# Attention in pairs of query blocks and fp32 pieces of one kind side by side, in a one-core kernel for a hybrid attention and retention layer

## The chip, the cores and the metric

One core of a Trainium2 chip runs the whole layer as one program. Its engines are TensorE (PE, the matrix engine), VectorE (DVE), ScalarE (ACT), GpSimd (POOL) and SyncE (SP, which issues nearly all DMAs). The metric is the device time of one execution in microseconds (us). Three runs of the kernel before took 1841.9, 1842.5 and 1843.4 us.

## The reference: what is computed

One layer of inference for 512 prompt tokens, 16 learned meta tokens ahead of them, and 8 samples of 4 new tokens each, which share all weights. Cut to what matters here:

```python
u = rms_norm(h, norm_g) @ w_in                    # 2048 -> 12800 columns, split into ten parts
qa, ka = rope(rms_norm(qa)), rope(rms_norm(ka))   # 16 query heads, 4 key heads, 64 wide
s = qa @ ka.T * 64 ** -0.5                        # keys: meta tokens, block before, own block
m = max(max(s), sink); p = exp(s - m)
o_a = (p / (sum(p) + exp(sink - m))) @ va         # samples: meta tokens, 128 cached keys, own 4
o_r = ((qr @ kr.T) * decay) @ vr + (qr @ S) * d   # retention, 8 heads, chunks of 128 tokens
S = g * S + (kr * wk).T @ vr                      # first S from the meta tokens
o_r = group_norm(o_r) * gn_g + gn_b
y = sigmoid(ga) * ((o_a * silu(za)) @ w_pa) + sigmoid(gr) * ((o_r * silu(zr)) @ w_pr)
out = h + y @ w_o
```

Everything is fp32. Outputs are the layer's result for prompt and samples, the last 128 keys and values, and the retention states.

## The kernel before

**Layout.** Activations stand with the model dimension on the partitions, 16 tiles of 128 (`XH`, `XL`), and tokens along the free dimension: 512 prompt, 32 sample, 16 meta. fp32 products are made from fp32r halves: `split` (L156) writes a high half on ACT and the rest on DVE, and a product is high x high + high x low + low x high. A matmul that reads true fp32 (transposes `tr` through L154, the products with `po`, `spo`, `ri`, `ru0`, `rx`) is not split; such a product shows as two instructions in the profile, a transpose as one.

**The stream of work.** `run_jobs` (L504) goes through jobs, 128 output columns of a weight matrix each: key, value, gate and query columns of attention, then the retention's, then gates and output projections in Strassen-like pairs (`Pair`, `pp`). For each the weights come by `run_load` into `wraw`, `run_split` makes `wspl`, and `run_mm` issues the matmuls into `pproj`, six per contraction step. After each step a clock ticks (`clock[0] += 1`) and `side_step` (L479) lets one waiting generator go on. These generators are the side work: attention heads (`pair_side` and one `block_side` for each of a head's four query blocks), samples (`sample_work`, `sample_side`), retention heads (`ret_side`), and the last residual adds (`out_side`). `yield n` puts a generator off by n ticks; `D2`, `D3`, `D4`, `DQ` (L120) are such distances, and at most `NACT` generators are active. So the order on each engine is fixed by the ticks, not by readiness, and an engine waits in order. The side work shares four PSUM banks (`psb`); the jobs have two double banks (`psmain`).

**The opening** is `start` (L246). It loads x in four token blocks and the samples with the meta tokens (`xext`), squares them (`sq`), takes the power on POOL and scales (`norm`), transposes (`make_x`, first for tokens 0 to 255, `half` 0, later for the rest), and runs the first job in two halves of tokens (`cuts`). `j1.ahead` steps of the second job are run on its first half alone. A table `plan` says behind which step the squares and `norm` of a block go.

**Attention.** `block_side` makes the scores of one block for the two heads of a pair (`psc`, four matmuls), masks and reduces on DVE, Exp on ACT (L732), scales on DVE (L739), transposes (`pT`), multiplies with the values (`po`, 64 output partitions per head) and transposes the meta columns (`pM`).

**Samples.** For each sample `sample_work` multiplies each of four key heads' 32 columns with the cached values (L837) and with the new ones (L838), 16 instructions in the profile; `sample_side` then transposes the sum (`pf`).

**The end.** `out_pair` (L1521) starts `out_side` behind the last step of a pair: ten transposes (`pout`), the residual adds and three stores.

Of the kernel before, what the change touches and what calls it, by code (L numbers as in the profile page):

```python
# [110 lines left out]
def hybrid_step(ctx: ExitStack, tc: tile.TileContext, A, O):  # L111
# [6 lines left out]
    NACT = 4  # L118
    LAG = 2
    D2, D3, D4, DQ = 2, 4, 3, 5  # L120
# [92 lines left out]

    def norm(i):
# [3 lines left out]
        nc.vector.tensor_reduce(out=r, in_=ss[:, i], axis=AX.X, op=ALU.add)  # L218
        rsqrt(r, r, 1.0 / D, 1e-6, 1)
# [26 lines left out]
    def start(j0, j1):  # L246
# [10 lines left out]
        load_ext()  # L257
        load_x(3)
        run_load(j1, 1)
# [5 lines left out]
        for i in range(2):  # L265
            for c in range(4):
                sq(i, c)
            norm(i)
        for j in (j0, j1):
            j.cuts = ((0, 256), (256, TF))  # L270
# [3 lines left out]
        plan = {2: "20 21", 4: "22 23", 6: "n2", 9: "40 41", 10: "42 43", 11: "n4", 14: "30 31", 15: "32 33"}  # L274
        for k in range(NK):
# [4 lines left out]
            for o in plan.get(k, "").split():  # L280
                if o[0] == "n":
                    norm(int(o[1]))
# [12 lines left out]
        for k in range(j1.ahead):  # L295
            run_mm(j1, k, (0,))
        for k in range(NK):
# [3 lines left out]
            if k in (8, 13):  # L301
                run_split(j1, {8: 2, 13: 3}[k])
# [24 lines left out]
    class Job:  # L327
        def __init__(self, w, c0, nk, rhs, n, evac, pre=None, need=None, kdone=None):
            self.w, self.c0, self.nk, self.rhs, self.n, self.evac = w, c0, nk, rhs, n, evac
            self.pre, self.need, self.kdone, self.cuts, self.ahead = pre, need, kdone, None, 0  # L330
            self.banked, self.tile = False, None
# [110 lines left out]
    def run_split(job, s, eng=nc.vector):  # L442
# [5 lines left out]
        wt = spl.tile([P, 2, 4, P], F32R, tag="spl", name="wspl")  # L448
        hi, lo = wt[:, 0], wt[:, 1]
# [177 lines left out]
    def k_side(n, raw):  # L627
# [5 lines left out]
        for i in range(4):  # L633
# [3 lines left out]
            if i < 3:  # L637
                nc.tensor.transpose(o[:, c + P:c + 144], kt[NS:48, 4], ident[NS:48, NS:48])
        tr(pe[:, :48], kt[:48, 4], 48)
# [40 lines left out]
    def pair_side(i, raw, get_sz):  # L680
# [8 lines left out]
        tr(pe[:, :NS], kt[:NS, 4], NS)  # L689
# [15 lines left out]
        for blk in range(4):  # L705
            side_add(block_side(i, blk, Q, st, get_sz))

    def block_side(i, blk, Q, st, get_sz):
        g = i // 2
        nkeys = 272 if blk else 144  # L710
        c0 = 144 * (blk - 1) if blk else 0
        m0 = 0 if blk else 144
        ko, mo = (144, P) if blk else (0, P)
        tt = slot(name="ptile")
        pt3 = r3(tt[:, :2 * nkeys], nkeys)
        mx = sm.tile([P, 2], F32, name="mx")
# [860 lines left out]
```

## Time and profile before

| what | value |
|---|---|
| three runs | 1841.9, 1842.5, 1843.4 us |
| the profiled execution | 1842.4 us, its span 1840.5 us |
| mean granted TensorE clock | 0.997 |
| PE busy | 1810.9 us, 14483 instructions |
| PEld (weight loads) busy | 1767.5 us |
| DVE, ACT, POOL busy | 1219.8, 731.4, 173.5 us |
| PE waits above 0.5 us in total | for `xin` 9.5, gains 7.2, `xh` 2.0, `xl` 1.8 + 1.0, `vmt` 1.1, `ptile` 0.7, `kt` 0.6, `wspl` 0.6 us |

The span runs from the first to the last instruction of the profiled execution; the rest of its time lies around it. Matmuls overlap, so the time one holds the queue is read from the start of the next, not from its own length: of `pproj` with 272 columns each takes about 0.29 us and a new one starts every 0.125 us. A row of the timeline has its start, its length, the engine, the line, the tiles (written <- read), rows x columns of the stationary operand, the moving operand's shape, and a count. A bracket gives the idle time before it and what ended it.

### The profile page before, as it was taken

To read this page: it belongs to the slowest core of one execution; us is meant where nothing else is said; L and a number is where in the kernel's file an instruction comes from. 1 tells how busy PE (TensorE), PEld (TensorE's weight loads), DVE (VectorE), ACT (ScalarE), POOL (GpSimd) and SP (SyncE) were. 2 spreads that over 40 slices of the span, in tenths; PEclk is the share of its full clock that TensorE was granted. 3 is DMA by queue.
4 is the path that set the end of the run, shared out by engine and by line. 5 is a ranking of instruction groups with operands and counts; after the bars stand their busy time and mean duration, and the time that the engine had idled before them with its cause. 6 is when DMAs were issued, how large, how long until landed. Compare 5 with 4: busy or idle time off the path is not lost.

```text
span 1840.5 us, 35155 instructions
## 1 busy us (share of the span) xinstructions
PE 1810.9 (98%) x14483; PEld 1767.5 (96%) x14483; DVE 1219.8 (66%) x2191; ACT 731.4 (40%) x1297; POOL 173.5 (9%) x240
## 2 busy tenths in 40 slices
PE   5999999999999999999999999999999999999999
PEld 4999999988999999999999999999999999999998
DVE  5636666645556555545697767777676678799776
ACT  5535555433323222233344444444444333344332
POOL 1100101100223212222000000000000000120000
PEclk8999999999999999999999999999999999999999
DMA  6232133231534443434454554444447764564553
GB/s 189 73 99 64 52 103 85 75 106 42 180 103 130 133 132 110 126 108 137 146 149 141 151 148 126 117 123 127 143 140 251 228 184 146 153 177 129 141 141 96
DMA packets 358368, 239.53 MB, mean 130 GB/s; under 512 B 12320, under 2 KB 332224, under 8 KB 358176
## 3 DMA queue, kind: packets, MB, share of 16 engines
q1 hardware_dynamic: 358208, 237.29, 44.1%
q8 instruction: 114, 1.87, 0.4%
q14 instruction: 46, 0.38, 0.1%
HBM read 197.27 MB, written 41.88 MB: 130 GB/s over the span
## 4 chain that ended last, share of the span: by engine, by line
PE 92%; DVE 3%; DMA 2%; ACT 1%; issue 1%; SPq 1%; POOL 0%; DVEq 0%; ACTq 0%
PE pproj L471 43%; PE pp L410 38%; PE ro L1137 1%; PE pp L471 1%; DVE wspl L158 1%; PE po L764 1%; DMA qdc<-c_qdec 1%; PE pout L154 0%; PE pT L154 0%; DVE ml L158 0%; PE rso L1097 0%; PE px L154 0%; PE rsu L1103 0%; PE psc L721 0%; PE pM L154 0%
## 5 line engine op out<-in xcount | busy, mean ns | idle before, releaser
L471 PE MATMUL pproj<-xh,wspl 128*128 128x272 f32 (+3 forms) x3840 | 714.6, 295 | 2.0 <-ACT xh L242 2.0
L158 DVE TENSOR_TENSOR wspl<-wraw,wspl 128x512 fp32r<-128x512 f32 (+1 forms) x492 | 465.0, 950 | 218.4 <-ACT wspl L157 215.6
L471 PEld LDWEIGHTS pproj<-xh,wspl 128*128 128x128 f32 x3840 | 567.4, 190 | 11.1 <-issue 4.8
L157 ACT ACTIVATE wspl<-wraw 128x512 fp32r<-128x512 f32 (+1 forms) x492 | 389.0, 804 | 371.5 <-DVE wraw L368 156.7
L471 PE MATMUL pproj<-xl,wspl 128*128 128x272 f32 (+3 forms) x1920 | 405.1, 290 | 1.0 <-DVE xl L243 1.0
L471 PEld LDWEIGHTS pproj<-xl,wspl 128*128 128x128 f32 x1920 | 305.4, 189 | 1.8 <-DVE xl L243 1.8
L410 PE MATMUL pp<-xfh,wspl 128*128 128x272 f32 x1280 | 246.2, 287 | 0.0
L410 PEld LDWEIGHTS pp<-xfh,wspl 128*128 128x128 f32 x1280 | 202.7, 188 | 0.0
L410 PE MATMUL pp<-xh,wspl 128*128 128x272 f32 x960 | 187.6, 288 | 0.0
L410 PE MATMUL pp<-xfl,wspl 128*128 128x272 f32 x640 | 162.8, 287 | 0.0
L410 PEld LDWEIGHTS pp<-xh,wspl 128*128 128x128 f32 x960 | 153.0, 188 | 0.0
L410 PE MATMUL pp<-fh,wspl 128*128 128x272 f32 x768 | 146.3, 288 | 0.2 <-ACT wspl L157 0.2
L410 PE MATMUL pp<-xl,wspl 128*128 128x272 f32 x480 | 123.0, 288 | 0.0
L410 PEld LDWEIGHTS pp<-fh,wspl 128*128 128x128 f32 x768 | 121.2, 188 | 0.6 <-ACT wspl L157 0.3
L410 PEld LDWEIGHTS pp<-xfl,wspl 128*128 128x128 f32 x640 | 120.7, 189 | 0.0
L410 PE MATMUL pp<-fl,wspl 128*128 128x272 f32 x384 | 98.1, 288 | 0.0
L410 PEld LDWEIGHTS pp<-xl,wspl 128*128 128x128 f32 x480 | 90.3, 188 | 0.0
L471 PE MATMUL pproj<-fh,wspl 128*128 128x272 f32 x512 | 84.9, 287 | 0.0
L368 DVE TENSOR_TENSOR wraw<-wraw 128x1024 f32<-128x1024 f32 x64 | 78.0, 1219 | 0.0
L410 PE MATMUL pp<-ofh,wspl 128*128 128x272 f32 x384 | 75.3, 290 | 0.0
L410 PEld LDWEIGHTS pp<-fl,wspl 128*128 128x128 f32 x384 | 72.3, 188 | 0.0
L471 PEld LDWEIGHTS pproj<-fh,wspl 128*128 128x128 f32 x512 | 72.2, 188 | 0.0
(314 smaller groups left out, 2445.9 us busy)
## 6 DMA issues: line engine op xcount, KB each, us to landing
wraw<-w_in SPq DMA_DIRECT2D x200, 512.0 KB
wraw<-w_branch_ret SPq DMA_DIRECT2D x32, 512.0 KB
wraw<-w_out SPq DMA_DIRECT2D x32, 512.0 KB
state<-state_ret SPq DMA_DIRECT2D x16, 512.0 KB
o_ret_sample<-state SPq DMA_DIRECT2D x16, 512.0 KB
wraw<-w_branch_attn SPq DMA_DIRECT2D x16, 512.0 KB
m1l<-m_scr SPq DMA_DIRECT2D x20, 272.0 KB
r_scr<-rprime SPq DMA_DIRECT2D x16, 272.0 KB
```

The costliest lines, as they stand in the source:

```text
L157: nc.scalar.activation(out=hi, in_=src, func=AF.Copy)
L158: eng.tensor_tensor(out=lo, in0=src, in1=hi.bitcast(F32), op=ALU.subtract)
L368: eng.tensor_tensor(out=out, in0=a, in1=b, op=ALU.add)
L410: nc.tensor.matmul(job.ps[bank], w[:, k], job.rhs(form, k)[q], start=fresh and i == 0, stop=i == len(seq) - 1, skip_group_check=True)
L471: nc.tensor.matmul(ps[h][:, :c1 - c0], w, x[:, c0:c1], start=a, stop=e)
L764: nc.tensor.matmul(o, src, PT[:, j * 256 + rh:j * 256 + rh + P], start=("s", j) not in st, stop=False, skip_group_check=True)
L1137: nc.tensor.matmul(o, w[:, cs], x, start=q == 0, stop=q == 5)
```

## The change

- **Blocks in pairs.** `block_side` takes two query blocks: both blocks' scores, one maximum and one sum for four columns, four Exp, two transposes' tiles, then `po` of both and both `pM` side by side. Distances become D2 = 3, D3 = 5, D4 = 5, and three generators are active, not four.
- **Samples.** The values become the stationary operand at full width: two products of 32 columns per sample. What belongs to the new tokens is collected (`spx`) and multiplied by two products at the end. The transposes `pf` go.
- **Shapes.** In `pair_side` and `k_side` the transpose of the extra tokens is a full 128 x 128 one, and the three 16-row ones stand in a row.
- **Retention.** The scores `ri` go up beside `rk`, `rva` of both halves stands with `rvb` and `rx`, `rot` of both halves together. The first state comes from three fp32r products in place of one fp32 product (`kmt`, `vmt` are replaced by `kml`, `vml`).
- **Opening.** `norm` is cut into `rstd` (sum and power) and the scaling. The low halves of six weight pieces are made on POOL, not on DVE; the third piece of the second job is split earlier than before. `j1.ahead` is 16, not 8, for which two pieces of the second job take tiles of `kk` (`spare`). Its second weight load is issued ahead of the fourth block of x.
- **Last stores.** `out_last` takes the place of `out_side` in the last pair: it starts one step earlier, with a delay of 4 ticks, and stores in five pieces.

```diff
-    NACT = 4
+    NACT = 3
-    D2, D3, D4, DQ = 2, 4, 3, 5
+    D2, D3, D4, DQ = 3, 5, 5, 5
...
+    def rstd(i):
+        r = xrs[:, i:i + 1]
+        nc.vector.tensor_reduce(out=r, in_=ss[:, i], axis=AX.X, op=ALU.add)
+        rsqrt(r, r, 1.0 / D, 1e-6, 1)
...
+        run_load(j1, 1)
         load_x(3)
-        run_load(j1, 1)
...
+        j1.spare = 2
...
-        plan = {2: "20 21", 4: "22 23", 6: "n2", 9: "40 41", 10: "42 43", 11: "n4", 14: "30 31", 15: "32 33"}
+        plan = {4: "20 21", 7: "22 23", 9: "r2", 10: "n2 40 41", 12: "42 43", 13: "r4 30 31", 14: "n4 32", 15: "33"}
...
             if k in (1, 5, 8):
-                run_split(j0, {1: 1, 5: 2, 8: 3}[k])
-            if k in (11, 13):
-                run_split(j1, {11: 0, 13: 1}[k])
-        norm(3)
+                run_split(j0, {1: 1, 5: 2, 8: 3}[k], nc.gpsimd)
+            if k in (9, 11, 13):
+                run_split(j1, {9: 0, 11: 1, 13: 2}[k], nc.gpsimd)
+        rstd(3)
         for k in range(NK - LAG, NK):
             run_mm(j0, k, (0,))
+        j1.ahead = 16
+        run_split(j1, 3)
+        norm(3)
+        for k in range(j1.ahead):
+            run_mm(j1, k, (0,))
         for k in range(3):
             make_x(k, 1)
-        j1.ahead = 8
-        for k in range(j1.ahead):
-            run_mm(j1, k, (0,))
...
-        tr(pe[:, :NS], kt[:NS, 4], NS)
+        tr(pe[:, :P], kt[:, 4])
...
-        for blk in range(4):
-            side_add(block_side(i, blk, Q, st, get_sz))
+        for b0 in (0, 2):
+            side_add(block_side(i, b0, Q, st, get_sz))
...
+        for bi, blk in enumerate(blks):
+            for src, rh in ((V4v[:, max(blk - 1, 0), gs], 0), (V4v[:, blk, gs], P)):
+                if rh == 0 and blk == 0:
+                    continue
+                for j in range(2):
+                    o = po[64 * j:64 * j + 64, blk * P:blk * P + P]
+                    nc.tensor.matmul(o, src, PTs[bi][:, j * 256 + rh:j * 256 + rh + P],
+                                     start=("s", j) not in st, stop=False, skip_group_check=True)
+                    st["s", j] = True
         pM = psb("pM")
-        tr(pM[:, :P], pc.rearrange("p v j c -> p (v j c)"))
+        for bi in range(2):
+            tr(pM[:, P * bi:P * bi + P], pcs[bi].rearrange("p v j c -> p (v j c)"))
...
-            for g in range(4):
-                o = po[32 * g:32 * g + 32, 64 * b:64 * b + 64]
-                nc.tensor.matmul(o, PT[:, 32 * g:32 * g + 32], vcv[:, bb, 64 * g:64 * g + 64], start=True, stop=False)
-                nc.tensor.matmul(o, PT[:48, P + 32 * g:P + 32 * g + 32], vx[:, 64 * g:64 * g + 64],
-                                 start=False, stop=True)
+            for q in range(2):
+                nc.tensor.matmul(pov[:, q, b], vcv[:, bb, P * q:P * q + P], ptv[:, q, :, 0:16],
+                                 start=first and q == 0, stop=False, skip_group_check=True)
...
+        for q in range(2):
+            nc.tensor.matmul(po[:, 256 * q:256 * q + 256], vx[:, P * q:P * q + P], st["px"][:48, 256 * q:256 * q + 256],
+                             start=False, stop=True, skip_group_check=True)
...
-        nc.tensor.matmul(pu[:, :256], kmt[96:128], vmt[96:128])
+        for q, (w, x) in enumerate(((kst, vst), (kst, vml), (kml, vst))):
+            nc.tensor.matmul(pu[:, :256], w[96:128], x[96:128], start=q == 0, stop=q == 2)
...
+    def out_last(n, y, x):
...
+        for b in range(2):
+            for j in range(2):
+                tr(pt[:, 0, 256 * b + P * j:256 * b + P * j + P], y[j][:, P * b:P * b + P])
+        yield 3
+        nc.vector.tensor_tensor(out=x[0][:, :512], in0=pt[:, 0], in1=x[0][:, :512], op=ALU.add)
+        nc.sync.dma_start(O["y_prompt"][0, 0:256, cs].rearrange("(b p) c -> p b c", p=P), r3(x[0][:, :512], 256))
+        for j in (1, 0):
+            while not done.get("last") and j == 0:
+                yield 1
...
+            nc.sync.dma_start(ysm[:, n * P + P * j:n * P + P * j + P], x[2][:NS, c])
...
+            if n == NK - 2:
+                if s == 5:
+                    side_add(out_last(n, t["y"], t["x"]), 4)
+                if s == 6:
+                    done["last"] = True
+            elif s == 6:
                 side_add(out_side(n, t["y"], t["x"]), 4)
```

**Where instructions move.** Three places; in each the rows of before come first, then those of the change. A row is the line, the operation, written <- read, and the shape.

TensorE, attention of one head pair: `po` is the product with the values, `pM` the meta columns' transpose, `pproj` the projection that runs meanwhile.

```order
L764 MATMUL po<-PT,v4a 64x128 x2
L154 MATMUL pM<-ident,pc 128x128
L471 MATMUL pproj<-xh,wspl 128x272 x2
L471 MATMUL pproj<-xl,wspl 128x272 x2
L471 MATMUL pproj<-xh,wspl 128x272 x2
L764 MATMUL po<-PT,v4a 64x128 x4
L154 MATMUL pM<-ident,pc 128x128
L471 MATMUL pproj<-xh,wspl 128x272 x2
L471 MATMUL pproj<-xl,wspl 128x272 x2
L471 MATMUL pproj<-xh,wspl 128x272 x2
L764 MATMUL po<-PT,v4a 64x128 x4
L154 MATMUL pM<-ident,pc 128x128
```

```order
L786 MATMUL po<-PT,v4a 64x128 x6
L154 MATMUL pM<-ident,pc 128x128 x2
L479 MATMUL pproj<-xh,wspl 128x272 x2
L479 MATMUL pproj<-xl,wspl 128x272 x2
L479 MATMUL pproj<-xh,wspl 128x272 x2
L786 MATMUL po<-PT,v4a 64x128 x8
L154 MATMUL pM<-ident,pc 128x128 x2
```

Four blocks' `po` and `pM` (the fourth stands 22 rows further in the program before) are now two groups; between a head's last `psc` and its `pT` of the second pair stand 60 matmuls of `pproj`.

VectorE, in the opening's loop: `xrs` is the sum that the scaling of `xin` needs, `xl` the low half of a transposed x tile, `xjunk` the squares, `wspl` a weight piece's low half.

```order
L243 SCALAR_TENSOR_TENSOR xl<-px,gains,xh 128x256
L158 TENSOR_TENSOR wspl<-wraw,wspl 128x512
L243 SCALAR_TENSOR_TENSOR xl<-px,gains,xh 128x256
L218 TENSOR_REDUCE xrs<-xss 128x1
L198 TENSOR_SCALAR xrs<-xrs 128x1
L225 TENSOR_SCALAR xin<-xin,xrs 128x512 x3
L243 SCALAR_TENSOR_TENSOR xl<-px,gains,xh 128x256 x2
L158 TENSOR_TENSOR wspl<-wraw,wspl 128x512
```

```order
L246 SCALAR_TENSOR_TENSOR xl<-px,gains,xh 128x256 x3
L211 SCALAR_TENSOR_TENSOR xjunk,xss<-xin 128x512
L246 SCALAR_TENSOR_TENSOR xl<-px,gains,xh 128x256 x2
L216 TENSOR_REDUCE xrs<-xss 128x1
L198 TENSOR_SCALAR xrs<-xrs 128x1
L246 SCALAR_TENSOR_TENSOR xl<-px,gains,xh 128x256
L228 TENSOR_SCALAR xin<-xin,xrs 128x512 x3
L211 SCALAR_TENSOR_TENSOR xjunk,xss<-xext 48x512
L246 SCALAR_TENSOR_TENSOR xl<-px,gains,xh 128x256 x2
```

The sum and the scaling, one behind the other before, have a tile's `xl` between them, and the weight pieces are no longer in the row.

The end of the program: TensorE, then SyncE's stores (`oy` is the last pair's result, `xres` and `xs` the residuals of prompt and samples).

```order
L410 MATMUL pp_11717<-mh,wspl 128x272
L410 MATMUL pp_11717<-ml,wspl 128x272
L410 MATMUL pp_11717<-mh,wspl 128x272 x8
L154 MATMUL pout<-ident,oy 128x128 x8
L154 MATMUL pout<-ident,oy 32x128 x2
```

```order
L415 MATMUL pp_11451<-mh,wspl 128x272
L415 MATMUL pp_11451<-ml,wspl 128x272
L415 MATMUL pp_11451<-mh,wspl 128x272 x8
L154 MATMUL pout<-ident,oy 128x128 x6
L154 MATMUL pout<-ident,oy 32x128
L154 MATMUL pout<-ident,oy 128x128 x2
L154 MATMUL pout<-ident,oy 32x128
```

```order
L363 DMA wraw<-w_out 128x8x128
L1500 DMA o_y_prompt<-xres 128x2x256 x2
L1504 DMA o_y_sample<-xs 32x256
L1481 DMA xres<-x_prompt 128x2x256 x2
L1484 DMA xs<-x_sample 32x256
L1500 DMA o_y_prompt<-xres 128x2x256 x2
L1504 DMA o_y_sample<-xs 32x256
```

```order
L1506 DMA xres<-x_prompt 128x2x256 x2
L1509 DMA xs<-x_sample 32x256
L1521 DMA o_y_prompt<-xres 128x2x256
L1532 DMA o_y_prompt<-xres 128x2x128
L1534 DMA o_y_sample<-xs 32x128
L1532 DMA o_y_prompt<-xres 128x2x128
L1534 DMA o_y_sample<-xs 32x128
```

All of the last pair's transposes still stand behind its last `pp`; there are five stores in place of three.

More of the change, by code (lines that the diff above doesn't have):

```diff
@@ L447, in run_split @@
         src = r3(job.raw[s // 2], P)[:, 4 * (s % 2):4 * (s % 2) + 4]
-        wt = spl.tile([P, 2, 4, P], F32R, tag="spl", name="wspl")
-        hi, lo = wt[:, 0], wt[:, 1]
+        if s < 4 - job.spare:
+            wt = spl.tile([P, 2, 4, P], F32R, tag="spl", name="wspl")
+            hi, lo = wt[:, 0], wt[:, 1]
+        else:
+            hi, lo = (r3(att.tile([P, TF], F32R, tag="kk", name="wspk", bufs=8)[:, :512], P) for _ in range(2))
         split(hi, lo, src, eng)
@@ L636, in k_side @@
             tr(o[:, c:c + P], kt[:, i])
-            if i < 3:
-                nc.tensor.transpose(o[:, c + P:c + 144], kt[NS:48, 4], ident[NS:48, NS:48])
-        tr(pe[:, :48], kt[:48, 4], 48)
+        tr(pe[:, :P], kt[:, 4])
+        for i in range(3):
+            c = 144 * (i % 2) + P
+            nc.tensor.transpose(pk[i // 2][:, c:c + 16], kt[NS:48, 4], ident[NS:48, NS:48])
         nc.vector.tensor_copy(kxT[:, n], pe[:, :48])
@@ new lines, in block_side @@
+        gs = slice(g * 64, g * 64 + 64)
+        blks = (b0, b0 + 1)
+        nk = [272 if blk else 144 for blk in blks]
+        mx, nmx, es, sums = (sm.tile([P, 4], F32, name=q) for q in ("mx", "nmx", "es", "sums"))
+        pts = []
+        for bi, blk in enumerate(blks):
+            nkeys = nk[bi]
+            c0 = 144 * (blk - 1) if blk else 0
+            m0 = 0 if blk else 144
+            pts.append(r3(slot(name="ptile")[:, :2 * nkeys], nkeys))
+            for j in range(2):
+                q = 2 * bi + j
+                ps = psb("psc")
+                lq = Q[j][:, blk * P:blk * P + P]
+                nc.tensor.matmul(ps[:, :nkeys], lq, KH[g][:, c0:c0 + nkeys], start=True, stop=False)
+                nc.tensor.matmul(ps[:, :nkeys], lq, KL[g][:, c0:c0 + nkeys], start=False, stop=True)
+                nc.vector.tensor_tensor_reduce(out=pts[bi][:, j], in0=ps[:, :nkeys], in1=mask[:, m0:m0 + nkeys],
+                                               scale=0.125, scalar=sinkb[:, 2 * i + j:2 * i + j + 1],
+                                               op0=ALU.add, op1=ALU.max, accum_out=mx[:, q:q + 1])
+            yield 2
@@ new lines, in block_side @@
+        nc.vector.tensor_scalar(out=nmx, in0=mx, scalar1=-1.0, scalar2=None, op0=ALU.mult)
+        nc.vector.tensor_tensor(out=es.rearrange("p (b j) -> p b j", j=2),
+                                in0=sinkb[:, 2 * i:2 * i + 2].unsqueeze(1).to_broadcast([P, 2, 2]),
+                                in1=mx.rearrange("p (b j) -> p b j", j=2), op=ALU.subtract)
+        for q in range(4):
+            nc.scalar.activation(out=pts[q // 2][:, q % 2], in_=pts[q // 2][:, q % 2], func=AF.Exp,
+                                 bias=nmx[:, q:q + 1], accum_out=sums[:, q:q + 1])
@@ L995, in ret_side @@
         tr(pe[:, :P], reps[0])
+        pi = psb("ri")
+        for c in range(4):
+            cs = slice(c * P, c * P + P)
+            nc.tensor.matmul(pi[:, cs], kT[:, cs], qT[:, cs])
         kwh, kwl = r2k(F32R, "kwh"), r2k(F32R, "kwl")
```

179 lines of the change are left out of this document (81 added, 98 removed).

## The prediction

> **What bounds the kernel now.** I read the page first: the span, then the chain of work that ended last.
>
> ```profile
> span 1840.5 us, 35155 instructions
> ...
> PE 92%; DVE 3%; DMA 2%; ACT 1%; issue 1%; SPq 1%; POOL 0%; DVEq 0%; ACTq 0%
> ```
>
> The profiled execution took 1842.4 us (1.9 around its span), 0.1 under the median of the runs shown, 1842.5; the sum is made against 1842.4. TensorE (PE) carries 92% of the chain, so what counts is how long each PE instruction holds the queue, and where PE waits. The table of PE's waits is short; its first row and the row on the softmax are these (total, times, longest):
>
> ```profile
> PE px L154 <- DVE xin L225: 9.5, 3, 3.3
> ...
> PE pT L154 <- DVE ptile L739: 0.7, 2, 0.5
> ```
>
> So there are two ways to gain: the waits, nearly all in the opening, and the small matmuls between the projection's (`pproj`, `pp`). The projection's own count is the same in both programs, 12624.
>
> **The small matmuls.** I price a group of small matmuls by what it adds to the stream: from the start of the projection row ahead of it to the start of the second row behind it, less what the two projection rows take alone. In the PE timeline (start, us) two rows of `pproj` with x2 stand 0.25 us apart, 0.125 a matmul.
>
> ```profile
> 250.91 0.44 PE L764 MATMUL po<-PT,v4a 128*64 128x128 f32 x4
> 251.28 0.33 PE L154 MATMUL pM<-ident,pc 128*128 128x128 f32 x1
> ...
> 286.80 0.41 PE L471 MATMUL pproj<-xh,wspl 128*128 128x272 f32 x2
> 287.14 0.66 PE L764 MATMUL po<-PT,v4a 128*64 128x128 f32 x8
> 287.73 0.33 PE L154 MATMUL pM<-ident,pc 128*128 128x128 f32 x1
> 287.81 0.49 PE L471 MATMUL pproj<-xh,wspl 128*128 128x272 f32 x2
> 288.15 0.29 PE L471 MATMUL pproj<-xl,wspl 128*128 128x272 f32 x1
> ```
>
> *Pairs of blocks (`po`, `pM`).* From 286.80 to 288.15 are 1.35 us; less 0.50 the group costs 0.85. Eight `po` take 0.59 to `pM`, four took 0.37, so four cost 0.22. What eight do not explain is 0.85 - 0.44 = 0.41, of which `pM`, a transpose, is 0.11 (below). So 0.30 is paid once per group for going into the half-width form and out: 0.34 in place of 0.25 stands both at its entry and at its exit. 32 groups become 16: 16 x 0.30 = **-4.8 us**; the bounds are 0.09 (one edge alone) and 0.30, so -1.4 to -4.8. Transposes show no such fee, so joining `pT`, `rva` and `rot` is worth 0.
>
> ```profile
> 402.17 0.30 PE L837 MATMUL spo<-kvc,sPT 128*32 128x64 f32 x2
> ...
> 403.99 0.44 PE L154 MATMUL pkc<-ident,kvc 128*128 128x128 f32 x2
> ...
> 468.23 1.05 PE L1012 MATMUL ri<-rot 128*128 128x128 f32 x8
> 469.04 0.50 PE L471 MATMUL pproj<-xh,wspl 128*128 128x280 f32 x2
> ```
>
> *Sample values (`spo`).* A sample's 16 instructions, all 32 columns wide, take 1.82 us, with the entry 1.92; eight samples 15.4. They become two full-width fp32 products, four instructions in the profile. Full-width fp32 runs in `ri` at 0.81 / 8 = 0.10 us, with the exit 0.11: four are 0.44, eight samples 3.5. Behind them come two products of 256 columns over 48 rows, which no row shows; by the `ru` rows below 1.4. The four transposes `pf` go (0.44). Sum 15.4 + 0.4 - 3.5 - 1.4 = **-10.9**. If a full-width instruction with so few columns cost what one of the 16 does (0.114) it is the same; if twice that, -7.3.
>
> ```profile
> 299.20 0.60 PE L154 MATMUL pq<-ident,kt 128*128 128x128 f32 x4
> 299.73 0.24 PE L154 MATMUL pqe<-ident,kt 32*128 32x32 f32 x1
> 299.91 0.52 PE L471 MATMUL pproj<-xh,wspl 128*128 128x272 f32 x2
> ```
>
> *Transposes of odd shape.* `pq` and `pqe` take 0.71 and an exit of 0.09, 0.80; five full ones 5 x 0.11 = 0.55. Eight heads: -2.0. In `k_side` three 16-row transposes stood between full ones, now in a row: per group two changes of shape fewer on each side and a full `pke`, an estimate by `pqe` of 0.6, twice: -1.2. Together **-3.2** (-2 to -4).
>
> ```profile
> 535.91 0.69 PE L1069 MATMUL ru<-vmt,kmt 32*128 32x256 f32 x2
> 536.54 0.53 PE L471 MATMUL pproj<-xh,wspl 128*128 128x280 f32 x2
> ```
>
> *First state (`ru`).* One fp32 product is two instructions: 0.63, with edges of 0.09 each 0.81. Three fp32r products replace it. At the pace of the projection (0.12) they are 0.36 + 0.18 = 0.54; at the pace of today's two, 1.14. I take the first, since fp32r passes once: 8 x -0.27 = **-2.2** (-2.2 to +2.6).
>
> **The opening.**
>
> ```profile
> 17.00:43.70 26.70, 18.97 (x104) 16.15 (x103) 18.93 (x49) 14.88 (x36) 1.80 (x4) 0.81 0.61 165
> ...
> 35.89 0.47 PE L154 MATMUL px<-ident,xin 128*128 128x128 f32 x1 [2.93 <-DVE xin L225]
> ```
>
> The first row is a stretch: from the first projection matmul (17.0) to the first of 304 columns (43.7) PE is busy 18.97 of 26.7 us; 0.81 is the granted clock. Idle are 7.7. A clock of 0.81 is 10 us at half speed (0.19 x 26.7 / 0.5); the wait of 2.93 lies among them, and the other 7 would take half, 3.5. So about 11 can be won at most. The change takes five weight subtractions off DVE (0.69 each, below) to POOL, runs `rstd` a step ahead of `norm`, so that DVE doesn't stand in front of POOL's power, and puts 24 more matmuls of the second job (24 x 0.12 = 2.9 us) where PE waited for `xin`. x3 arrives later, behind a 512 KB weight load, but its squares come only at the loop's end. What stays: the first two steps at half clock (three matmuls and two transposes each, 1.2 lost) and a lag of DVE. I take **-9**; ends -3 (only the extra matmuls) and -11.
>
> ```profile
> L158 DVE TENSOR_TENSOR wspl<-wraw,wspl 128x512 fp32r<-128x512 f32 x56 | 38.4, 688 | 25.0 <-ACT wspl L157 24.9
> ...
> L1027 POOL TENSOR_TENSOR innl<-inn,innh 128x512 fp32r<-128x512 f32 x8 | 10.3, 1288 | 15.6 <-ACT innh L1026 15.6
> ...
> 462.20 2.46 DVE L158 TENSOR_TENSOR wspl<-wraw,wspl 128x512 fp32r<-128x512 f32 x2
> ...
> 462.32 1.79 POOL L954 TENSOR_TENSOR rot<-rot,rtmp 128x544 f32<-128x544 f32 x1 [14.11 <-DVE rtmp L953]
> ```
>
> What speaks against: POOL needs 1.29 us for such a subtraction, and two DVE subtractions that ran beside a POOL one took 2.46 instead of 1.38. Six on POOL are 7.7 us; if they meet DVE's squares and scalings for half or more of that, DVE is 4 to 6 us later. [...]
>
> **The last stores.** (DVE, SP issue and PE, in order of time.)
>
> ```profile
> 1834.76 1.57 PE L154 MATMUL pout<-ident,oy 128*128 128x128 f32 x10
> 1834.96 0.44 DVE L429 TENSOR_TENSOR oy<-pp,oy 128x272 f32<-128x272 f32 x1 [2.54 <-PE pp L410]
> 1835.40 0.69 DVE L1499 TENSOR_TENSOR xres<-pout,xres 128x512 f32<-128x512 f32 x1
> ...
> 1836.12 1.36 SPq L1500 DMA_DIRECT2D o_y_prompt<-xres  x2
> ...
> 1837.57 0.41 SPq L1504 DMA_DIRECT2D o_y_sample<-xs  x1
> ```
>
> The new order lets the first transposes only after the last matmul of the step (its delay of 4 ticks is the step's whole length), so nothing is stored earlier. The first store is ready as before, at 1836.1; then SP issues five in place of three, some 0.45 apart (0.41 for one, and a gap): the last at 1837.9, not 1837.6. **+0.4** (-0.5 to +0.8).
>
> **New waits in attention.** Before, three of a head's four blocks came to Exp together and the fourth later; now all four come together.
>
> ```profile
> 276.15 0.41 ACT L732 ACTIVATE ptile<-ptile,nmx 128x144 f32<-128x144 f32 x1 [4.46 <-DVE nmx L729]
> ...
> 279.27 0.62 ACT L157 ACTIVATE wspl<-wraw 128x512 fp32r<-128x512 f32 x1
> ...
> 279.40 0.16 DVE L736 TENSOR_TENSOR sums<-sums,es 128x2 f32<-128x2 f32 x1
> 279.59 0.17 DVE L737 RECIPROCAL sums<-sums 128x2 f32<-128x2 f32 x1
> 279.80 0.63 DVE L739 TENSOR_SCALAR ptile<-ptile,sums 128x272 f32<-128x272 f32 x2
> ...
> L723 DVE CUSTOM_DVE_ANT_0 ptile<-psc,mask,sinkb 128x272 f32<-128x272 f32 (+1 forms) x56 | 23.4, 464 | 12.8 <-PE psc L722 12.8
> ```
>
> Three blocks' Exp took 3.12 us; four take about 4.1, with one weight split (0.6) 4.7. Then DVE scales the second pair: sum and reciprocal 0.4, 4 x 0.32. From the last `psc` to the second pair's `pT` the new order has 60 projection matmuls and six transposes, 60 x 0.125 + 6 x 0.11 = 8.2 us; two score reductions (0.46 each), Exp and scaling need 0.9 + 4.7 + 1.7 = 7.3, and a second split on either engine (0.6 to 0.7) uses most of the margin. Behind the waiting DVE instruction stand the next weights' subtractions, behind PE's wait the whole projection. I take **+3** (0.4 a head; 0 to 20). In retention I expect no cost: its groups keep their distances, and no wait of PE for a bank stood there before.
>
> **Sum:** 1842.4 - 4.8 - 10.9 - 3.2 - 2.2 - 9.0 + 0.4 + 3.0 = 1815.7, **1816 us**.
>
> **Rivals.**
> [...]
> - *`pT` waits every head*: 2.6 us eight times, 21 in place of 3: 1834. For it the thin margin of 0.9; against it, before had only 0.7 in all.
> - *The small matmuls keep their price*: half of `spo` and a third of `po` is won, 5.4 and 3.2 lost: 1825. It covers, too, that the change doesn't do what it says.
> - *Slower*: DVE, waiting in order for the eight Exp's sums, holds the subtractions of `wspl`, and the projection itself runs dry in attention. It decides from (26.7 + 3) / 8 = 3.7 us a head; with an Exp table load and two splits caught in between (some 4.2) it gives 34 in place of 3: 1847.
>
> **How the numbers follow.** Forecast 0.58, port 0.17, `pT` 0.12, price 0.09, slower 0.04. The range leaves out `pT` and the slower rival, 0.16, and takes in the others with the ends of the unknown costs: down to 1806 (opening -11, no new waits, the rest a little cheaper than taken) and up to 1830 (the price rival with +5 of waits). About 0.2% (3.7 us) is what a measurement of this kernel can tell from no change; within it only part of the slower rival falls: faster 0.95, same 0.01, slower 0.04.
>
> **What would show it.** `po` in groups of 6 and 8 with `pM` x2 costing 1.2 and 1.4; `spo` x4 in 0.44; the first 304-column matmul near 37.5 (43.7 - 9 + 2.9), with a granted clock of 1.0 from 20 on; PE's waits for `xin` inside that stretch gone; the last store issued near its end, five in a row. Wrong: a row of PE waits for `ptile` or `wspl` above 5 us.

## The result, and the profile after

The changed kernel takes 1820.1 us (median of 4 runs, 1818.8 to 1820.4), the kernel before 1842.9 beside it (1841.9 to 1843.4): a ratio of 0.9875, 95% interval 0.9858 to 0.9892. That is 22.8 us less; the forecast was 1816, 26.5 less than the runs shown then. The profiled execution took 1819.9 us, 22.5 under that of before.

The page of the changed kernel (span; busy time, share and instructions of PE; shares of the chain by engine):

```profile
span 1817.9 us, 34819 instructions
...
PE 1788.9 (98%) x14395; PEld 1763.9 (97%) x14395; DVE 1205.3 (66%) x2082; ACT 722.0 (40%) x1257; POOL 181.7 (10%) x246
...
PE 94%; DVE 3%; DMA 1%; issue 1%; ACT 1%; POOL 0%; SPq 0%; DVEq 0%; ACTq 0%
```

PE carries 94% of the chain now, 92% before. The table of PE's waits (total, times, longest), without `pg` (the first gains, 7.4) and the rows below 0.9:

```profile
PE px L154 <- DVE xin L228: 7.4, 2, 4.1
...
PE rx L1064 <- POOL qpad L1040: 5.1, 1, 5.1
PE pproj L479 <- ACT xh L245: 1.3, 1, 1.3
PE pproj L479 <- DVE xl L246: 1.2, 1, 1.2
PE pk L154 <- DVE kt L633: 0.9, 1, 0.9
```

Three things are to be seen. The softmax's `ptile` has no row at all, so the waits in attention that the forecast feared did not come. There is a new row of 5.1 us, for `rx` in retention, where the forecast had no cost. And the opening, from the first projection matmul to the first of 304 columns, has two waits left, for `xh` and `xl`, 2.5 us together; before it had five there, 7.5 us together (1.8, 0.4 and 0.4 for `xl`, 2.0 for `xh`, 2.9 for `xin`). The 7.4 for `xin` lie ahead of that stretch.

Since both programs have the same 12624 projection matmuls, the n-th of them can be compared between two traces. The difference says how much the kernel has won up to that place (start times in us; the n-th is counted from 0, so the 300th stands right behind the second of the two groups that transpose k):

| | before | after | difference |
|---|---|---|---|
| first projection matmul | 17.0 | 18.1 | +1.1 |
| first of 304 columns | 43.6 | 40.0 | -3.6 |
| 300th projection matmul (opening done) | 86.9 | 80.3 | -6.6 |
| 2600th (attention and samples done) | 474.9 | 444.1 | -30.8 |
| 2700th | 492.9 | 466.7 | -26.2 |
| last | 1834.6 | 1811.9 | -22.7 |
| end of the span | 1840.5 | 1817.9 | -22.6 |

Between the 2600th and the 2700th 4.5 us are lost again: that is the place of `rx`. From the 5400th on the difference changes by 0.4 alone.

**The groups.** In PE's timeline of the changed kernel (start, us) these are a pair of blocks, a sample, and the first state:

```profile
277.11 0.41 PE L479 MATMUL pproj<-xh,wspl 128*128 128x272 f32 x2
...
277.45 1.09 PE L786 MATMUL po<-PT,v4a 128*64 128x128 f32 x16
278.48 0.44 PE L154 MATMUL pM<-ident,pc 128*128 128x128 f32 x2
278.67 0.50 PE L479 MATMUL pproj<-xh,wspl 128*128 128x272 f32 x2
...
279.00 0.41 PE L479 MATMUL pproj<-xl,wspl 128*128 128x272 f32 x2
...
410.78 0.41 PE L479 MATMUL pproj<-xh,wspl 128*128 128x272 f32 x2
411.03 0.53 PE L863 MATMUL spo<-sPT,kvc 128*128 128x32 f32 x4
411.39 0.50 PE L479 MATMUL pproj<-xh,wspl 128*128 128x272 f32 x2
411.72 0.41 PE L479 MATMUL pproj<-xl,wspl 128*128 128x272 f32 x2
...
471.40 0.38 PE L1092 MATMUL ru<-vst,kst 32*128 32x256 f32 x1
471.62 0.28 PE L1092 MATMUL ru<-vml,kst 32*128 32x256 f32 x1
471.74 0.27 PE L1092 MATMUL ru<-vst,kml 32*128 32x256 f32 x1
471.95 0.53 PE L479 MATMUL pproj<-xh,wspl 128*128 128x280 f32 x2
```

The pair costs 279.00 - 277.11 = 1.89, less four projection matmuls (0.50) 1.39. The forecast's price (16 `po` at 0.055, two transposes at 0.11, one fee of 0.30) gives 1.40. The sample costs 0.94 - 0.50 = 0.44, as forecast. The first state's three products start 0.22 and 0.12 apart and the projection goes on 0.21 later, so the group is dearer than 0.54; over all 8 heads its median is 0.74, before 0.83.

**The opening.** A row of the table by stretches (us; busy time and instructions of PE, PEld, DVE, ACT, POOL; granted clock; DMA), from the first projection matmul to the first of 304 columns, then stretches in the opening and behind `rx`:

```profile
18.07:40.00 21.93, 19.38 (x127) 17.93 (x125) 18.08 (x43) 15.42 (x37) 10.64 (x10) 0.92 0.84 226
...
22.00:28.00 6.00, 5.42 (x45) 5.09 (x43) 5.02 (x13) 5.34 (x13) 4.13 (x4) 1.00 1.05 298
28.00:36.00 8.00, 6.04 (x35) 5.84 (x36) 7.40 (x18) 5.30 (x14) 4.13 (x4) 0.79 0.79 203
...
461.70:463.00 1.30, 1.23 (x5) 1.23 (x6) 0.55 (x1) 0.72 (x2) 1.30 (x3) 0.50 1.04 302
463.00:465.00 2.00, 2.00 (x11) 2.00 (x10) 0.14 (x1) 0.00 (x0) 1.92 (x3) 0.50 0.64 167
```

The stretch is 21.9 us long, 26.7 before, with 24 matmuls more in it; the clock is 0.92, not yet 1.0: it stands at 1.00 from 22 to 28 and at 0.79 from 28 to 36. What ran there is seen in the timeline (DVE, POOL and PE):

```profile
26.95 1.26 POOL L158 TENSOR_TENSOR wspl<-wraw,wspl 128x512 fp32r<-128x512 f32 x1
...
27.01 2.28 DVE L228 TENSOR_SCALAR xin<-xin,xrs 128x512 f32<-128x512 f32 x3
...
28.75 0.38 PE L479 MATMUL pproj<-xh,wspl 128*128 128x256 f32 x1 [1.33 <-ACT xh L245]
...
30.35 0.38 PE L479 MATMUL pproj<-xl,wspl 128*128 128x256 f32 x1 [1.21 <-DVE xl L246]
```

Three scalings that take 1.28 without a POOL subtraction beside them (experiment 5) took 2.28 beside one of 1.26: held up by 1.0, and on a scaling with one operand. A second set, at 33.1, took 2.29 beside one of 1.28. TensorE's two waits stand close by, but experiment 5 shows that they do not hang on this hold.

**The new wait.** SP's issues, POOL and PE around `rx` in the first retention head:

```profile
445.07 0.81 SPq L913 DMA_DIRECT2D o_win_k_sample<-cache_win_k  x1
445.92 0.70 SPq L913 DMA_DIRECT2D o_win_v_sample<-cache_win_v  x1
...
447.44 0.43 SPq L993 DMA_DIRECT2D qdc<-c_qdec  x1
...
460.01 1.26 POOL L1036 TENSOR_TENSOR qd<-rot,qdc 128x512 f32<-128x512 f32 x1 [10.38 <-DMA qdc<-c_qdec]
461.21 0.20 POOL L1040 COPY qpad<-rot 128x16 f32<-128x16 f32 x1
...
461.77 0.80 PE L1064 MATMUL rx<-qpad,rep 128*128 128x128 f32 x2 [5.13 <-POOL qpad L1040]
```

The row `qdc` of 64 KB is issued at 447.4, behind two window copies of 992 KB each, and lands at 460, 12.6 us later. POOL's `qd` waits for it, `qpad` stands behind `qd` in POOL's order though it doesn't need it, and `rx` needs `qpad`. In the kernel before the load was as late (issued at 462.8, `qd` began at 475.0), but `rx` stood behind two more yields and came when `qpad` was there. Behind the wait the clock is at half: 3.3 us at 0.50 up to 465, so the wait costs some 1.7 us more than its length (an estimate, 0.5 x 3.3).

### The profile page after: what moved, and what is told of

Read it like the earlier page. It is cut to its first block, busy times and chain, and to the rows that moved or that the text cites. A ratio compares the mean times of both kernels' runs of the same rounds, so it can differ in the third digit from the quotient of the medians.

```text
span 1817.9 us, 34819 instructions
## 1 busy us (share of the span) xinstructions
PE 1788.9 (98%) x14395; PEld 1763.9 (97%) x14395; DVE 1205.3 (66%) x2082; ACT 722.0 (40%) x1257; POOL 181.7 (10%) x246
## 4 chain that ended last, share of the span: by engine, by line
PE 94%; DVE 3%; DMA 1%; issue 1%; ACT 1%; POOL 0%; SPq 0%; DVEq 0%; ACTq 0%
PE pproj L479 45%; PE pp L415 38%; PE ro L1160 1%; PE pp L479 1%; DVE wspl L158 1%; PE po L786 1%; DMA qdc<-c_qdec 1%; PE pT L154 1%; DMA xin<-x_prompt 1%; PE px L154 1%; PE pout L154 0%; DVE ml L158 0%; PE rso L1120 0%; PE psc L735 0%; PE psc L734 0%
## 5 line engine op out<-in xcount | busy, mean ns | idle before, releaser
L479 PE MATMUL pproj<-xh,wspl 128*128 128x272 f32 (+3 forms) x3808 | 696.7, 294 | 1.3 <-ACT xh L245 1.3
L479 PEld LDWEIGHTS pproj<-xh,wspl 128*128 128x128 f32 x3808 | 559.3, 189 | 8.3 <-ACT xh L245 1.5
L373 POOL TENSOR_TENSOR wsum<-wraw 128x1024 f32<-128x1024 f32 x2 | 4.8, 2399 | 704.5 <-DMA m1l<-m_scr 698.1
```

What stands on the lines that cost most here:

```text
L373: eng.tensor_tensor(out=out, in0=a, in1=b, op=ALU.add)
L479: nc.tensor.matmul(ps[h][:, :c1 - c0], w, x[:, c0:c1], start=a, stop=e)
```

## The experiments

Times are medians beside the kernel before on the same chip (1842.1 to 1843.4). Since executions differ by up to 2 us in the pace of the projection alone, local effects are read from the n-th projection matmul.

**1. Window copies behind the first head's loads.**

```diff
-        copy_windows()
         yield 1
...
             Sts.append(r3(t, 256))
+        if h == 0:
+            copy_windows()
```

> The changed kernel with one edit: the two copies of the windows (about 1 MB each) are issued behind the loads of retention's first head instead of ahead of them. Theory: TensorE's new wait of 5.1 us at rx is a late load; the decay row qdc, issued right behind the two copies, landed 12.6 us after its issue, GpSimd's qd waited for it and qpad behind qd. Then qdc lands some 3 us after its issue, TensorE's wait for qpad goes, and the time is 1820 - 5 = 1815 us. Rival: rx simply stands too early in its step and the load would be late in any order, or the weights behind the copies come late instead: a wait of 3 us or more stays in TensorE's table and the time is 1818 to 1820.

Measured 1812.1 us, ratio 0.9832 (0.9818 to 0.9847). SP and POOL in its timeline:

```profile
446.17 0.42 SPq L992 DMA_DIRECT2D qdc<-c_qdec  x1
...
451.28 1.54 POOL L1037 TENSOR_TENSOR qd<-rot,qdc 128x512 f32<-128x512 f32 x1 [2.93 <-DMA qdc<-c_qdec]
```

`qdc` is there 5.1 us after its issue, not 12.6, and the wait for `qpad` is gone from PE's table. From the 2600th to the 2700th matmul this version wins 6.9 us: 5.1 of wait, the rest clock. Of the 8.2 between the two profiled executions (8.0 between the medians) the other 1.3 lie in the opening and are not the edit: the last part of the second block of x landed later in the profiled execution of the changed kernel (`px` for it began at 15.7 there; 14.5 to 14.9 in twelve of the fourteen profiles of this study). Whether the other three executions of the changed kernel had the late load isn't known. This version is the base of most runs that follow.

**2. `rx` put back.**

```diff
-        px = psb("rx")
-        nc.tensor.matmul(px[:, :P], reps[0], qp.rearrange("p a b -> p (a b)"))
         for n in range(2):
...
+        px = psb("rx")
+        nc.tensor.matmul(px[:, :P], reps[0], qp.rearrange("p a b -> p (a b)"))
         r = slice(96, 128)
```

> The changed kernel with one edit: rx goes back behind the two steps of the value halves, where it stood before the change. Theory: the wait of 5.1 us comes from the place of rx alone; some 6 ticks later (about 4.5 us and more) qpad is there, the wait goes, the load of qdc is as late as ever, and the time is 1815 us. Rival: the wait only moves (what is behind the late qd, the products of the query halves, becomes the wait), or rx alone between projection matmuls costs a switch again (8 x 0.3 = 2.4): 1817.5 to 1820.

Measured 1813.6 us, 0.984 (0.9824 to 0.9857). Its rows of PE's waits:

```profile
PE ru L1092 <- DVE vml L1076: 0.9, 1, 0.9
...
PE rx L1074 <- POOL qpad L1040: 0.2, 1, 0.2
```

The place of `rx` alone takes away 5.1 to 0.2; 0.9 come back one step further, and at the 2800th matmul it is 1.9 behind experiment 1. Both theories hold in part: the move made the wait, the late load is its cause.

**3. The two blocks' `po` apart.**

```diff
+        pM = psb("pM")
         for bi, blk in enumerate(blks):
...
-        pM = psb("pM")
-        for bi in range(2):
+            tr(pM[:, P * bi:P * bi + P], pcs[bi].rearrange("p v j c -> p (v j c)"))
```

> The changed kernel with one edit: inside each pair's step the order is po of the first block, its pM, po of the second block, its pM, so that the half-width form is entered and left twice, with as many instructions at the same place. Theory (a fee of 0.30 us per entry into and exit from the half-width form): 16 groups more, 16 x 0.30 = +4.8, 1825 us, and a group of 8 po and its pM apart costs 0.3 more. Rival (the gain came from fewer interruptions of the projection, not from the switches): at most +1, 1820 to 1821.

Measured 1824.1 us, 4.0 more. The same pair in its PE timeline:

```profile
278.05 0.41 PE L479 MATMUL pproj<-xh,wspl 128*128 128x272 f32 x2
278.39 0.66 PE L787 MATMUL po<-PT,v4a 128*64 128x128 f32 x8
278.98 0.33 PE L154 MATMUL pM<-ident,pc 128*128 128x128 f32 x1
279.23 0.66 PE L787 MATMUL po<-PT,v4a 128*64 128x128 f32 x8
...
280.24 0.41 PE L479 MATMUL pproj<-xl,wspl 128*128 128x272 f32 x2
```

2.19 - 0.50 = 1.69 against 1.39: 0.30 for one entry and exit more, as many instructions at the same place. Both kinds of group show it (1.70 for 1.40 and 1.48 for 1.18), 16 x 0.30 = 4.8. By the marks it loses 4.9 between the 300th and the 2600th matmul; the profiled executions differ by less, 3.6, because the late load of x is missing in this one. The fee is shown.

**4. The opening as before.**

```diff
-        j1.ahead = 16
-        run_split(j1, 3)
-        norm(3)
-        for k in range(j1.ahead):
-            run_mm(j1, k, (0,))
+        norm(3)
...
         for k in range(3):
             make_x(k, 1)
+        j1.ahead = 8
+        for k in range(j1.ahead):
+            run_mm(j1, k, (0,))
...
```

> The changed kernel with the opening as before the change (order of loads, norm in one piece, low weight halves on VectorE, 8 matmuls ahead), all else as changed. Theory from the two timelines (the first 304-column matmul came 3.75 us earlier, with 24 matmuls more ahead of it, 2.8 us): the opening won 6.6, so 1820 + 6.6 = 1826.7, with the first 304-column matmul at 43.8. Rival (the prediction's -9 stands and what is missing was lost elsewhere): 1829. Second rival (the later part of the kernel gives the gain back, since the next jobs' weights come at their own pace): 1820 to 1823.

Measured 1823.8 us, 3.7 more than the changed kernel. Its 300th matmul starts at 85.5, 5.3 later than in the changed kernel and 6.5 later than in experiment 1, which has the early load. So the opening is worth about 6.5, less the 1.3 of a late load in this one profile. The time shows less, near what the second rival had, but not for its reason: at the 2700th matmul it is still 5.3 behind, and then comes back bit by bit to 4.1 at the last, since the same matmuls run 0.1% faster in this execution. The transposes of k stand here without the wait for `kt` (groups of 1.53 us, twice); in the changed kernel one of the two waits 0.9 and costs 2.69.

**5. The low weight halves of the opening on VectorE.**

```diff
-                run_split(j0, {1: 1, 5: 2, 8: 3}[k], nc.gpsimd)
+                run_split(j0, {1: 1, 5: 2, 8: 3}[k])
...
-                run_split(j1, {9: 0, 11: 1, 13: 2}[k], nc.gpsimd)
+                run_split(j1, {9: 0, 11: 1, 13: 2}[k])
```

> The version with the window copies late (1812.1) with one edit: the six low weight halves of the opening are made on VectorE instead of GpSimd. [...] What GpSimd's help is worth is only the difference: the first 304-column matmul comes 1 to 2 us later than 38.8, and the time is 1813 to 1814. Rival (the prediction's step, the help counts in full): first 304-column matmul at 42 or later, with the wait for xin of some 2 to 3 us back and a half clock behind it, 1816. Second rival (the help is harm): 1811 or less.

Measured 1810.5 us. The scalings take 1.28 again:

```profile
26.84 1.28 DVE L228 TENSOR_SCALAR xin<-xin,xrs 128x512 f32<-128x512 f32 x3
```

The 300th matmul comes 0.57 later than in experiment 1, less than the 1 to 2 us that were expected, and than the first rival had. The second rival's time, 1811 or less, came, but not through the opening: the 1.9 us are gained bit by bit over the remaining 1700 us, at a pace 0.1% faster, on another chip, and beside the kernel before the two ratios hardly differ (0.9826, interval 0.9812 to 0.9841). Six subtractions moved to GpSimd are worth 0.6 us here, not the 4.1 (6 x 0.69) that they take on VectorE. TensorE's waits in that stretch stay without the hold, 1.2 for `xh` and 1.2 in three parts for `xl`, and so does the granted clock:

```profile
28.00:36.00 8.00, 6.83 (x40) 6.44 (x41) 7.28 (x22) 5.42 (x15) 2.01 (x3) 0.79 0.74 201
```

So the hold is real, but neither these waits nor the clock behind them come from it alone: on VectorE the subtractions (0.69 each) take time in its place.

**6. Eight steps ahead instead of sixteen.**

```diff
-        j1.ahead = 16
+        j1.ahead = 8
```

> The version with the window copies late (1812.1) with one edit: 8 instead of 16 matmul steps of the second job run ahead, so that 24 matmuls (24 x 0.118 = 2.8 us) go back behind the first job's second half. Theory: they fill time in which TensorE would wait for the scaled x3 (its first piece is there at 36.8, TensorE would be done at 34.3): the wait for xin comes back with some 2.6 us, the projection is 2.6 us later from then on and, with a half clock behind a wait of that length, up to 4: 1815 to 1816. Rival: the wait is hidden by other work (the transposes of the first job's second half are there in time): below 1, 1812 to 1813.

Measured 1823.2 us, 11 more: both theories missed. The wait came back as expected (2.59 us), but 10.4 us are lost by the 300th matmul. By stretches, this version and then experiment 1:

```profile
42.00:50.00 8.00, 8.00 (x28) 5.78 (x27) 2.16 (x5) 2.34 (x5) 0.00 (x0) 0.50 0.23 66
50.00:60.00 10.00, 10.00 (x36) 7.39 (x35) 3.20 (x6) 2.80 (x6) 0.00 (x0) 0.50 0.00 0
```

```profile
42.00:50.00 8.00, 8.00 (x48) 6.25 (x48) 4.09 (x9) 4.07 (x8) 0.00 (x0) 1.00 0.23 66
```

The same stage (three matmuls of 304 columns, then two transposes and one of 48 rows) ran at 1.00 in experiment 1, where it was entered so, and stayed at 0.50 for some 20 us here, where it was entered behind the wait, though PE was busy throughout. Its first to last 304-column matmul take 34.6 us in place of 22.0.

**7. Eight steps, but dense matmuls behind the wait.**

```diff
-        j1.ahead = 16
+        j1.ahead = 8
         run_split(j1, 3)
         norm(3)
-        for k in range(j1.ahead):
-            run_mm(j1, k, (0,))
         for k in range(3):
             make_x(k, 1)
+        for k in range(j1.ahead):
+            run_mm(j1, k, (0,))
```

> The version with the window copies late (1812.1) with one edit: 8 steps of the second job run ahead, and the first transposes of the first job's second half stand ahead of them, not behind (the order of before the change). With 8 steps behind the wait for xin the granted clock stayed at 0.50 from 42 to 60 us and the kernel lost 10.4. Theory (it is the stretch of 304-column matmuls with their transposes that doesn't get the clock back once a wait has cost it; dense matmuls do): here 24 dense matmuls lie between the wait and that stretch, the clock is back at 1.0 within some 6 us, the stretch takes about 22 us in place of 34.6, and the 300th projection matmul comes 3 to 4.5 us later than with 16 steps: 1815 to 1817. Rival (the number of steps run ahead decides, the cold clock comes in any order): 10 later, 1822.

Measured 1818.2 us. The wait is longer, the stage is at 1.00:

```profile
38.00:42.00 4.00, 4.00 (x20) 3.62 (x19) 1.07 (x2) 0.81 (x2) 0.00 (x0) 0.52 0.07 19
42.00:50.00 8.00, 8.00 (x52) 6.43 (x50) 3.03 (x6) 3.09 (x6) 0.00 (x0) 1.00 0.09 23
```

The 300th matmul is 5.8 later than in experiment 1, not 10.4 (4.5 was expected at most; the wait is 6.0 here). Behind the wait stand dense matmuls here, and the clock is back at 1.00 at 42, some 6 us later; in experiment 6 it stayed at 0.50 up to 60 in the stage with transposes. Experiment 6 has the other half of this in its own trace: the clock had fallen there too, to 0.79 from 28 to 36, and was back after 3.4 us at 0.50 (0.21 x 8 / 0.5), a stretch of matmuls of 0.58 to 0.63 us with no transpose between them. What the two runs show of the order is its price, 4.6 us; why the clock came back in one and not in the other they don't show.

**8. The first state's products issued twice** (the second three write the same place anew, so the result is the same).

```diff
+        for _ in range(2):
             for q, (w, x) in enumerate(((kst, vst), (kst, vml), (kml, vst))):
```

> The version with the window copies late with one edit: the three products of the first state are issued twice, the second time into the same place from the start, so that the result is the same. Their group costs 0.74 now, and the prediction took 0.54 = 3 x 0.12 + 0.18. Theory (a product costs 0.12 and the switch into and out of 32 rows costs 0.38, not 0.18): three more cost 0.36, the group 1.10, 1812.1 + 8 x 0.36 = 1815. Rival (each product on 32 rows costs 0.25): three more cost 0.74, the group 1.48, 1818.

Measured 1815.5 us (a single run; its second block of x landed late too). PE's timeline:

```profile
464.64 0.27 PE L1094 MATMUL ru<-vst,kml 32*128 32x256 f32 x1
464.76 0.28 PE L1094 MATMUL ru<-vst,kst 32*128 32x256 f32 x1
```

Three more cost 2.8 us over 8 heads by the projection's marks, 0.35 a head: 0.12 each. So a product is as cheap as forecast, and the switch into and out of 32 rows costs 0.74 - 0.36 = 0.38, not 0.18.

**9. Less delay in attention.**

```diff
-    D2, D3, D4, DQ = 3, 5, 5, 5
+    D2, D3, D4, DQ = 3, 3, 5, 5
```

> The version with the window copies late with one edit: the delay from the exponentials to the scaling and from there to pT is two ticks (some 1.5 us) shorter in all (D3 3 in place of 5). Theory (the margin in attention is as thin as the prediction had it, and the waits of 3 us stayed out by half a microsecond): in a head's second pair the first scaled block is there 0.55 us ahead of pT now, so pT waits some 0.9 us in each of 8 heads, 1812.1 + 7 = 1819, with a row of TensorE's waits for ptile near 7. Rival (the margin is wider, the prediction had counted too much into it): no wait above 1 us in all, 1812. Second rival (VectorE stands in order behind the exponentials and the weights' halves come late): TensorE waits for wspl in attention, 1825 and more.

Measured 1826.5 us, 14.3 more. PE's waits:

```profile
PE pT L154 <- DVE ptile L756: 6.5, 8, 0.9
PE rx L1065 <- POOL qpad L1041: 3.5, 2, 1.9
```

The waits for `ptile` are those expected: the margin is thin. The time is near the second rival's, but its row, a wait for `wspl` in attention, is not there. The cost of the waits isn't as expected: the groups of `pT` and the transposes that went with them cost 9.8 us more in all (behind its first wait each `pT` follows the scalings one by one), and in two retention heads `rx`, now earlier against its loads, waits again, 4.1 by its groups.

**10. Warming products.**

```diff
+        pw = psetup.tile([P, 512], F32, tag="px", name="pwarm")
+        wz = vz.rearrange("p a b c -> p (a b c)")
+        for _ in range(5):
+            nc.tensor.matmul(pw, wz[:, :P], wz)
```

> The version with the window copies late with one edit: five fp32 products of zeros by zeros (128x512) that nobody reads are put on TensorE's queue behind the transpose of the gains, in the time in which it waits for the first rows of x (7.5 to 14.7 us). Theory (TensorE's half clock limits the first steps): the granted clock is 1.0 from the first projection matmul on and not from 19.7, and the 300th projection matmul comes 1 to 1.5 us earlier, 1811. Rival (VectorE and ScalarE set the pace of the first steps): the clock is 1.0 there all the same, and the time is 1812. Second rival (the products hold up the first transposes): some 0.5 later.

Measured 1810.8 us, 0.9829 (0.9813 to 0.9846). The 300th matmul comes 0.9 us earlier: near the theory. The first projection matmul, in PE's timeline of this version and of experiment 1:

```profile
16.79 0.39 PE L483 MATMUL pproj<-xh,wspl 128*128 128x256 f32 x1
```

```profile
17.09 0.58 PE L479 MATMUL pproj<-xh,wspl 128*128 128x256 f32 x1
```

It takes 0.39 and not 0.58, though the column of the granted clock has 1.00 for 17 to 20 in both. The trace's record of the clock starts only at 19.3 in experiment 1, at 11.2 here, and the column shows 1.00 where there is no record: for the first matmuls of a run the durations tell.

**11. Sample values as before.**

```diff
-            for q in range(2):
-                nc.tensor.matmul(pov[:, q, b], vcv[:, bb, P * q:P * q + P], ptv[:, q, :, 0:16],
-                                 start=first and q == 0, stop=False, skip_group_check=True)
+            for g in range(4):
+                o = po[32 * g:32 * g + 32, 64 * b:64 * b + 64]
+                nc.tensor.matmul(o, PT[:, 32 * g:32 * g + 32], vcv[:, bb, 64 * g:64 * g + 64], start=True, stop=False)
...
```

> The version with the window copies late with one edit: the sample values as before the change (16 products of 32 columns for each sample, a copy, and four transposes at the end). Theory (the time goes by instructions of TensorE, and the groups in the two traces differ by 11.7 us): 1812.1 + 11.7 = 1823.8. Rival (the prediction's other end: a full-width product of so few columns costs twice what the groups seem to show, or the old group lay beside other work): +7.3 or less, 1819.4.

Measured 1824.8 us, 12.7 more; 1.2 of it is a wait of `rke` for POOL's `rep` that only this version has. The theory's 11.7 stands.

**12. The best version.** Experiments 1 and 10, with the two low halves that ran beside scalings back on VectorE.

```diff
-                run_split(j1, {9: 0, 11: 1, 13: 2}[k], nc.gpsimd)
+                run_split(j1, {9: 0, 11: 1, 13: 2}[k], nc.gpsimd if k == 11 else nc.vector)
```

> The window copies late, the five warming products, and two of the six low weight halves of the opening (those that ran beside the scaling of x2 and of the 48 extra rows) back on VectorE. Theory (a scaling that a GpSimd subtraction holds takes 1.0 us more, the same subtraction on VectorE takes 0.69): the two scalings take 1.28 again, the 300th projection matmul comes 0 to 0.6 us earlier than with the warming products alone, 1810.5. Rival (VectorE sets the pace of the opening by its sum of work, so that the two halves cost it 1.4): 0 to 0.8 later, 1811.5.

Measured 1810.5 us (5 runs, 1810.3 to 1810.9), 0.9826 (0.9813 to 0.9839). The two scalings take 1.28 and 1.27, the 300th matmul comes 0.13 earlier than in experiment 10. It beats both kernels; nearly all of that is experiment 1, and beside the kernel before it can't be told from experiments 1, 5 and 10.

## Why the prediction was right, and where it was wrong

The time lies in the range, and 4.2 us over the forecast when profiled execution is set against sum. Some of that closeness is luck: in the terms below 12.0 us were won less than forecast (retention 6.9, opening 2.7, first state 1.5, `pk` 0.9) and 7.8 more (waits in attention 3.7, all others 4.1), and the two nearly offset each other.

| term of the sum (us) | forecast | measured | from |
|---|---|---|---|
| pairs of blocks | -4.8 | -4.8 | groups; experiment 3 |
| sample values | -10.9 | -11.7 | groups; experiment 11 |
| odd transposes `pq`, `pk` | -2.0, -1.2 | -2.1, -0.3 | groups |
| first state | -2.2 | -0.7, and a wait of 1.2 less | groups; experiment 8 |
| opening | -9.0 | -6.3 (-7.6 without the late load) | the 300th matmul, less `pk` |
| last stores | +0.4 | +0.1 | end of the span less last matmul |
| waits in attention | +3.0 | -0.7 | PE's table |
| retention | 0 | +6.9 | experiment 1 |
| rest, put to no term | | -1.7 | |
| sum | -26.7 | -22.5 | |

- **Small matmuls: right, by the mechanism.** The fee per switch is what the forecast read from one row, 0.30, and full-width instructions cost 0.11 with 32 columns too. The two products over 48 rows took 1.26, 1.4 was taken. So the rival of kept prices fell.
- **First state: the price of a product was right, the fee was mis-sized.** An fp32r product is one instruction of 0.12 in the rows (experiment 8). The forecast took two edges of 0.09; there are four of about 0.1 in the changed kernel's rows (starts 0.35 for 0.25 and 0.22 for 0.12 apart going in, 0.21 for 0.12 and 0.36 for 0.25 coming out), 0.38 in all by experiment 8. The wait of the first head's `ru` for `vmt`, 1.1 in PE's table of before, went with the fp32 copy; the forecast hadn't counted it.
- **Odd transposes:** `pk` would have won 1.5 (experiment 4, 2.27 to 1.53 twice); a new wait of 0.9 for `kt` takes most of it.
- **Opening: 1.4 too much (2.7 with the late load), and in part for another reason than given.** The forecast gave weight to five subtractions off VectorE; experiment 5 prices them at 0.6. The chances have a case "port" (0.17): no run shows a port; what the runs showed in its place are three scalings that take 2.28 beside a POOL subtraction and 1.28 without one, which would have been the answer had the rest been worth nothing. What wins is the order: sixteen steps ahead, for which the forecast had 2.9 us of filled wait, close the wait for `xin`, and so the clock stays at 1.00 in the stage in which it stood at 0.50 for some 20 us in experiment 6. With eight steps in the order of before 5.8 of the 6.5 are gone (experiment 7), with eight in the new order more than all of it (experiment 6). The forecast had no price for the clock in the stage behind that wait, and what the earlier `rstd` and the order of loads are worth each was not tested apart.
- **Waits in attention: none came, and the 0.7 of before went.** The rows of the second pair in the changed kernel, DVE's scalings and `pT`:

```profile
270.11 1.21 DVE L756 TENSOR_SCALAR ptile<-ptile,sums 128x272 f32<-128x272 f32 x4
...
271.00 1.04 PE L154 MATMUL pT<-ident,ptile 128*128 128x128 f32 x8
```

The first scaled half is there 0.55 us ahead of its transpose. The reckoned margin of 0.9, "most" of which a second split was to use, was right; the 3 us were taken out of caution, and experiment 9 shows how near the rival of waits in every head was.
- **Retention: the step that failed.** "In retention I expect no cost: its groups keep their distances." They don't: `rx` moved ahead of two yields, past the time at which its operand is made. The change's order shows that move; the forecast asked whether a bank was free, not whether POOL's chain behind a load was done. 6.9 us, the largest error.
- **Last stores:** +0.1 for +0.4; five stores in a row at the end, as said.

The rest is nearly accounted for by groups, priced as above. Before had short waits that the new kernel lacks, and they cost more than their idle time: five of `pM` 0.9 together, three of `psc` 0.9, and the two of `ptile` 0.5 more than the 0.7 in the table. Retention's joined groups are 0.4 cheaper. Against this, the same projection matmuls, away from any group and wait, took 0.8 longer in all in the changed kernel's execution. That makes -1.9 for the -1.7.

## What to carry to other kernels

When instructions are gathered into one group, ask of each that comes earlier what makes its operand and which load stands ahead of that; a small load issued behind two large copies came late (`qdc` 12.6 us after its issue behind two of 992 KB, 5.1 without them). What short instructions of another shape cost was not set by their size here: count the entries and exits (`po` 0.30, `ru` 0.38 a group) and the instructions themselves (a sample's 16 became 4, at 0.11 each). Fill a wait ahead of a stage like that of the 304-column matmuls, which stood at 0.50 for some 20 us behind a wait of 2.6, or put dense matmuls between the two (5.8 us lost in place of 10.4).

## What the runs showed of the hardware

- A wait of 2.6 us ahead of a stage that mixes matmuls and transposes left the granted clock at 0.50 for some 20 us of busy PE; the same stage entered at 1.00 kept it (0.50 from 42 to 60 us in experiment 6, 1.00 in experiments 1 and 7). A wait of 5.1 us, that for `rx`, ahead of dense matmuls cost 3.3 us at half clock (0.50 from 461.7 to 465 in the changed kernel).
- The clock also fell, to 0.79 from 28 to 36 us, in the changed kernel behind two waits of 1.3 and 1.2 us close together, none longer, and again to 0.79 in experiment 5, behind waits of 0.6, 1.2, 0.2 and 0.4.
- Two executions differed by about 0.1% in the pace of the same matmuls without any wait (1.9 us over 1700, experiments 1 and 5, on two chips), and the kernel before spread over 3.4 us on one chip, so edits worth less than 2 us are read from marks in the trace rather than from the time.
